# A fp32 decoder layer on one core: MLP operands two pairs to an instruction, norm scratch and load order changed

## The chip, the core and the metric

The kernel runs on one core of a Trainium2 chip. The core has five engines, each with its own instruction queue: TensorE (PE), VectorE (DVE), ScalarE (ACT), GpSimd (POOL) and SyncE (SP, which here issues most DMA transfers). The metric is device time in microseconds for one launch, the median of the runs. All times in the text are microseconds unless marked ns.

## The reference, cut to what matters

One decoder layer, 2048 tokens of 1024 features, all in fp32. A token mixer comes first; it is not touched by the change. The rest is:

```python
x = x + merged @ w_o                                   # mixer: merged is its output
h = rmsnorm(x, g_mlp)
x = x + jnp.square(jax.nn.relu(h @ w_ff1)) @ w_ff2     # 1024 -> 4096 -> 1024
h = rmsnorm(x, g_ple)
x = x + jax.nn.sigmoid(h @ w_ple_gate) * (p @ w_ple_proj)
return rmsnorm(x, g_final)
```

## The kernel before

**Splitting.** Every fp32 operand of a product is split into a rounded part and a remainder (`split`, L1101 to L1103): ACT casts (L1102), then DVE or POOL subtracts the cast from the source (L1103). `mm3` (L133) makes a product from three matmuls: high by high, high by low, low by high. So each 128x512 operand costs one ACT instruction and one DVE or POOL instruction, which stand in the profile as `op<-hr`, `op<-w` and so on under L1102 and L1103.

**Seven products.** Both MLP products are done by a scheme with seven instead of eight half-size products, P1 to P7, on sums and differences of the blocks. The tokens are two blocks (`blk`) of 1024. The combinations of the activations are called A11, A12, S1, S2, S3, A22 and S4, those of the weights are formed by a subtraction in place, and the order is P1, P2, P5, P6, P7, P4, P3.

**First product (about 1660 to 2390).** For each block 16 pairs of column tiles; a pair (`pair`) has 84 matmuls, 12 to each of the seven products. The activations stand split in SBUF (`home`: hA, hS, yx, big), the weight operands come from `combine`. The additions and the squared ReLU after it (L1276, L1282) run on DVE and POOL on tiles of the ring `t2` (7 buffers), and the results go to DRAM (`rD`, L1288). While block 0's pairs run, `heads1` prepares block 1: it loads x (`hr`, a ring of two buffers, L1108), normalizes it (`norm_tile`: a Square on ACT with its sum, L160, the result going to an unused tile `junk` that is taken from the t2 ring; a chain of small DVE instructions for the reciprocal root, L165 and L149 to L155; a DVE product, L173), transposes it on PE (L137), and puts the combinations into DRAM (`hD`). At the last pair of block 0 `fill_home` loads these into `hr` and splits them into the home tiles, as soon as the last matmul on each is done: half on DVE, half on POOL, 128x1024 each.

**Second product (about 2390 to 3041).** For each block four chunks of the 4096 hidden columns, in each chunk seven products: 56 steps of 48 matmuls. For the step after the present one, `operands` loads the activations (`hr`, 1 MB, L1367), splits them on ACT and POOL, forms the weight combination from `w` tiles (L1375 for P5, L1377 for P6, L1379 for P7, L1381 for P4, all on POOL) and splits it on ACT and DVE; four pairs (activations, weights) to a step, each pair one tile of the ring `op`, of 6 + 10 tiles, that is, two steps. The weights come as 64 loads of 512 KB (`load_w2`, L1354). Each product is added to its accumulators `accP` (L1440 on ACT for first chunks, else L1442 on DVE); in the last chunk of a block the accumulators are combined (L1448) and put to DRAM (`x2D`, L1451), for block 1 from ACT's queue. The accumulators of P2, P4 and P3 start from the residual (`accP<-x1D`, L1420), loaded at the first P1 of a block. PSUM: a step uses four `d` banks or two `rp` and two `rc`, by turns.

**Gate stage (3041 to the end).** Gate weights are loaded (L1488) and split to `wg`, the input is normalized (`norm_in`, L1395, L160, L173) and turned (`turn_in`), then gate, embedding and the last norm.

**What sets the order.** PE's order is the order in which the code is written. That of DVE, ACT, POOL and SP is set by a scheduler when the kernel is built, which may hoist an instruction: the first two `norm_in` of the gate stage, written near the end of the second product, stand on DVE at the switch from block 0 to block 1. Each engine works through its own row in order; an instruction that waits holds all that stand behind it.

Of the kernel before, what the change touches and what calls it, by code (L numbers as in the profile page):

```python
# [98 lines left out]
def hybrid_kernel(ctx, tc, consts, x, p, g_mix, w_in, mu_shift, w0, w_decay_up, a0, w_aaa_up,  # L99
# [101 lines left out]
    with ExitStack() as c1:  # L201
# [886 lines left out]
        ring = dict(n=0, a=6, b=6)  # L1088

        def optile():  # L1090

            n = ring["n"] % (ring["a"] + ring["b"])
            ring["n"] += 1
            if n < ring["a"]:
                return hx.tile([P, 2, 512], FR, name="op", tag="op", bufs=ring["a"])
            return ring["pool"].tile([P, 2, 512], FR, name="op", tag="op", bufs=ring["b"])
# [66 lines left out]
        def combine(pool, pr, wrb, tmp):  # L1163
# [10 lines left out]
            def op(nm, src, eng):  # L1174
                t = optile().rearrange("p s (k n) -> p s k n", n=P)
                split((t[:, 0], t[:, 1]), src, eng)
                ops[nm] = t
# [88 lines left out]
    def prod(ops, nm, last):  # L1266
        ps = pps()
        h = home[FIRST[nm]]
        for k in range(4):
            mm3(ps, (ops[nm][:, 0, k, :], ops[nm][:, 1, k, :]), (h[:, 0, k, :], h[:, 1, k, :]), k == 0, k == 3)  # L1270
        if last:
            fill_home(FIRST[nm])
        return ps
# [71 lines left out]
    ring.update(pool=f3, b=10, n=0)  # L1345
    w2v = w_ff2[0].rearrange("(k p) c -> p k c", p=P)
    lo, hi = slice(0, 512), slice(512, D)

    def load_w2(c):
        w = {}  # L1350
        for e in range(2):
            for p_ in range(KC):
                w[p_, e] = g3.tile([P, D], F32, name="w2", tag="w2", bufs=12)
                SP.dma_start(out=w[p_, e], in_=w2v[:, 2 * (c * KC + p_) + e, :])  # L1354
        return w
# [9 lines left out]
    def operands(blk, c, nm, w):  # L1365
# [3 lines left out]
        for p_ in range(KC):  # L1369
            a = optile()  # L1370
            split((a[:, 0, :], a[:, 1, :]), raw[:, p_, :], POOL)
            e, o = w[p_, 0], w[p_, 1]
            b11, b12, b21, b22 = e[:, lo], e[:, hi], o[:, lo], o[:, hi]
            if nm == "P5":
                POOL.tensor_tensor(b11, b12, b11, ALU.subtract)  # L1375
            elif nm == "P6":
                POOL.tensor_tensor(b11, b22, b11, ALU.subtract)  # L1377
            elif nm == "P7":
                POOL.tensor_tensor(b12, b22, b12, ALU.subtract)  # L1379
            elif nm == "P4":  # L1380
                POOL.tensor_tensor(b21, b21, b11, ALU.subtract)  # L1381
# [8 lines left out]
    hts, xts = {}, {}  # L1390
# [21 lines left out]
    for n, (blk, c, nm) in enumerate(seq):  # L1412
        cur = nxt
        g = blk * NCH + c
        if nm == "P1":
            if c == 0:

                for a, e, ns in (("P2", 0, lo), ("P4", 1, lo), ("P3", 0, hi)):
                    for j in range(4):
                        SP.dma_start(out=accs[a][j], in_=x1D[rows_of(blk, e, j), ns])  # L1420
# [3 lines left out]
        if n + 1 < len(seq):  # L1424
# [4 lines left out]
            nxt = operands(b_, c_, nm_, w2[b_ * NCH + c_])  # L1429
        pss = [dps() for _ in range(4)] if n % 2 == 0 else [rps(), rps(), cps(), cps()]  # L1430
# [6 lines left out]
        for j in range(4):  # L1437
# [12 lines left out]
            def put(k, e, ns):  # L1450
                (ACT if blk + 1 == NBLK else SP).dma_start(out=x2D[rows_of(blk, e, j), ns], in_=s[k])  # L1451
# [28 lines left out]
    wgv = w_ple_gate[0].rearrange("(k p) c -> p k c", p=P)  # L1480
    wpv = w_ple_proj[0].rearrange("(k p) c -> p k c", p=P)
# [3 lines left out]
    def weights(view, res, pool, n, ks, nm):  # L1485

        raw = hr()
        SP.dma_start(out=raw[:, 0:len(ks), :], in_=view[:, ks[0]:ks[-1] + 1, (lo, hi)[n]])  # L1488
# [118 lines left out]
```

## Time and profile before

| | us |
|---|---|
| runs | 3300.75, 3304.99, 3310.25; median 3304.99 |
| profiled execution | 3303.2 |
| its span | 3301.4 |
| PE busy in the span | 3054.8 (93%) |
| DVE, POOL, ACT busy | 2455.9 (74%), 1653.8 (50%), 1336.2 (40%) |

The profile is of one execution. A row of the order of time reads: start, length, engine, line, operation, output <- inputs, shapes, count of merged instructions, and in brackets how long the engine had been idle and what released it. A row of the list of waits reads: who waited, for which engine's which tile and line, total, times, longest. L numbers are lines of the kernel before; the helpers `split` and `mm3` appear under their own lines.

### The profile page before, as it was taken

Reading aid. Unit: us, or ns where it says so; the run is one execution under the profiler, and the core shown is the slowest. Engines: PE = TensorE matmul, PEld = TensorE weight load, DVE = VectorE, ACT = ScalarE, POOL = GpSimd, SP = SyncE. Lnnn points to the kernel's source line nnn. Section 1 sums busy time; section 2 is a strip of 40 time slices with the busy share of each in tenths; the row PEclk is TensorE's granted clock in tenths of the full one; section 3 lists DMA queues with packets and bytes.
Section 4 is the critical chain, followed back from the end, with each engine's and each line's share of the span. In section 5 each row is a group of like instructions: output and inputs, shape, how many; then the busy total and the mean of one; then the engine's idle time right before and its main releaser. Section 6 shows DMA issues by size and latency. Waiting matters only on the chain. (4 is left out here: it accounts for less than half of the span.)

```text
span 3301.4 us, 44294 instructions
## 1 busy us (share of the span) xinstructions
PE 3054.8 (93%) x14409; PEld 2492.0 (75%) x14409; DVE 2455.9 (74%) x5424; ACT 1336.2 (40%) x2774; POOL 1653.8 (50%) x1657
## 2 busy tenths in 40 slices
PE   7999989999999998788989889899989998999998
PEld 6777777777878786677777667688878886887787
DVE  4479888788888878875477777776657697668665
ACT  4445655455455444432233223222244434443332
POOL 4545444444334434531245456655589887885000
PEclk9999999999999999899999999899999999999999
DMA  7876767765666567767755455544464464335331
GB/s 246 241 225 196 244 202 233 237 216 192 216 211 218 188 205 238 246 213 264 273 193 177 148 177 190 181 153 147 169 227 153 142 217 177 141 128 177 127 115 67
DMA packets 423219, 636.41 MB, mean 193 GB/s; under 512 B 174222, under 2 KB 286412, under 8 KB 391756
## 3 DMA queue, kind: packets, MB, share of 16 engines
q1 hardware_dynamic: 420684, 629.39, 57.7%
q10 hardware_dynamic: 2304, 4.20, 0.3%
q8 instruction: 114, 1.87, 0.2%
q14 instruction: 117, 0.96, 0.1%
HBM read 439.49 MB, written 193.99 MB: 192 GB/s over the span
## 5 line engine op out<-in xcount | busy, mean ns | idle before, releaser
L133 PE MATMUL d<-big,wf 128*128 128x512 f32 (+1 forms) x3288 | 849.7, 406 | 19.1 <-DVE wf L244 8.9
L133 PEld LDWEIGHTS d<-big,wf 128*128 128x128 f32 x3288 | 609.5, 192 | 157.7 <-DVE wf L244 11.4
L1103 DVE TENSOR_TENSOR op<-w,op 128x512 fp32r<-128x512 f32 x224 | 287.4, 1295 | 139.2 <-ACT op L1102 137.8
L1103 POOL TENSOR_TENSOR op<-hr,op 128x512 fp32r<-128x512 f32 x224 | 331.2, 1494 | 95.5 <-ACT op L1102 95.5
L133 PE MATMUL d<-op 128*128 128x512 f32 x1344 | 314.6, 393 | 12.6 <-POOL op L1103 8.9
L133 PEld LDWEIGHTS d<-op 128*128 128x128 f32 x1344 | 253.4, 189 | 69.2 <-POOL op L1103 9.3
L1102 ACT CAST op<-hr 128x512 fp32r<-128x512 f32 x224 | 139.3, 622 | 323.2 <-PE rc L133 109.8
L872 DVE TENSOR_TENSOR Xtmp<-Xt,At 128x16 f32<-128x16 f32 (+15 forms) x512 | 242.8, 474 | 9.3
L1103 POOL TENSOR_TENSOR op<-wr,op 128x512 fp32r<-128x512 f32 x96 | 141.5, 1483 | 206.3 <-ACT op L1102 206.3
L133 PE MATMUL d<-yx,wf 128*128 128x512 f32 x768 | 206.9, 416 | 22.7 <-ACT yx L390 15.7
L133 PE MATMUL d<-wf,big 128*128 128x512 f32 x768 | 200.8, 415 | 26.1 <-DVE t2k L611 13.8
L133 PE MATMUL d<-wg,op 128*128 128x512 f32 x768 | 187.0, 399 | 11.3 <-ACT wg L1102 11.0
L133 PEld LDWEIGHTS d<-wf,big 128*128 128x128 f32 x768 | 146.6, 196 | 64.1 <-DVE t2k L611 17.4
L1276 POOL TENSOR_TENSOR t<-t,t 128x512 f32<-128x512 f32 x128 | 189.4, 1490 | 9.8 <-issue 5.6
L133 PEld LDWEIGHTS d<-yx,wf 128*128 128x128 f32 x768 | 147.3, 198 | 59.8 <-ACT yx L390 17.4
L133 PE MATMUL rp<-op 128*128 128x512 f32 x672 | 173.5, 393 | 13.9 <-DVE accP L1442 12.3
L133 PEld LDWEIGHTS d<-wg,op 128*128 128x128 f32 x768 | 147.1, 192 | 46.4 <-ACT wg L1102 11.6
L1102 ACT CAST op<-wr 128x512 fp32r<-128x512 f32 x192 | 110.0, 618 | 166.9 <-DMA wr<-in_w_ff_dram 113.1
L133 PE MATMUL rc<-op 128*128 128x512 f32 x672 | 171.7, 391 | 0.0
L244 POOL TENSOR_TENSOR wf<-wr,wf 128x640 fp32r<-128x640 f32 (+2 forms) x69 | 120.5, 1747 | 78.5 <-ACT wf L241 74.3
L133 PEld LDWEIGHTS rp<-op 128*128 128x128 f32 x672 | 126.9, 190 | 42.0 <-issue 12.7
L875 DVE TENSOR_REDUCE Xt<-Xtmp 128x8 f32<-128x16 f32 (+15 forms) x512 | 147.3, 288 | 9.2
(319 smaller groups left out, 6396.4 us busy)
## 6 DMA issues: line engine op xcount, KB each, us to landing
wf<-wc SPq DMA_DIRECT2D x131, 1024.0 KB, 5.4
wc<-wf SPq DMA_DIRECT2D x50, 1024.0 KB, 6.3
wr<-in_w_ff_dram SPq DMA_DIRECT2D x64, 512.0 KB, 4.4
w<-in_w_ff_dram SPq DMA_DIRECT2D x64, 512.0 KB, 4.2
wr<-in_w_in_dram SPq DMA_DIRECT2D x51, 512.0 KB, 4.3
zD<-t2k SPq DMA_DIRECT2D x96, 256.0 KB, 3.9
zs<-zD SPq DMA_DIRECT2D x32, 640.0 KB, 6.4
At<-aD SPq DMA_DIRECT2D x32, 512.0 KB, 5.1
```

What stands on the lines that cost most here:

```text
L133: PE.matmul(out_, lhsT, rhs, start=start, stop=stop, **kw)
L244: eng.tensor_tensor(wf[:, 1, c], raw[:, c], hi.bitcast(F32)[:, c], ALU.subtract)
L872: DVE.tensor_tensor(tmp[:, :, :, 0:n], Xt[:, :, 0:n].unsqueeze(2).broadcast_to([P, MCOL, FS, n]), At[:, 0:n, r:n].rearrange("p s r -> p r ...
L875: DVE.tensor_reduce(Xt[:, :, r:n].unsqueeze(3), tmp[:, :, :, 0:n], AX.X, ALU.add)
L1102: ACT.copy(out=dst[0], in_=src)
L1103: eng.tensor_tensor(dst[1], src, dst[0].bitcast(F32), ALU.subtract)
L1276: eng.tensor_tensor(out_, a, b, op)
```

## The change

1. The ring `op` has tiles of twice the size and half their number (3 + 3 in the first product, 3 + 5 in the second). In the first product two operands share a tile (`ophalf`). In the second, `operands` treats two pairs at once: casts, subtractions and weight combinations are 128x1024 instead of 128x512, half as many. The weight loads are 32 of 1 MB.
2. The weight combinations of P5 and P6 move from POOL to DVE; those of P7 and P4 stay on POOL.
3. `fill_home` runs at high priority, and gives DVE 128x1024 and 128x512, POOL 128x512.
4. The norm of `heads1` squares in two halves into a scratch tile of its own (`jk`), with one more DVE addition of the two sums (L1125), and no longer takes a tile of the t2 ring. Its product is now L1126.
5. The residual loads of P4 and P3 move from the first P1 to the first P6 of a block.
6. Block 1's stores to `x2D` are issued by SP instead of ACT.
7. The first raw gate weights are loaded in the last but one step (`graws`); `turn_in` uses one double tile.

```diff
-        ring = dict(n=0, a=6, b=6)
+        ring = dict(n=0, a=3, b=3)
...
-                norm_tile(pool, x_, gb, x_, junk)
+                if junk:
+                    norm_tile(pool, x_, gb, x_, junk)
+                    continue
+                ss = pool.tile([P, 2], F32, name="nss2", bufs=2)
+                for n in range(2):
+                    jk = pool.tile([P, 512], BF16, name="jk", bufs=1)
+                    ACT.activation(out=jk, in_=x_[:, n * 512:(n + 1) * 512], func=AF.Square, accum_out=ss[:, n:n + 1])
+                DVE.tensor_tensor(ss[:, 0:1], ss[:, 0:1], ss[:, 1:2], ALU.add)
+                DVE.scalar_tensor_tensor(x_, x_, rstd(pool, ss[:, 0:1], 1, "n"), gb, op0=ALU.mult, op1=ALU.mult)
...
-        for k, eng in ((slice(0, 2), DVE), (slice(2, 4), POOL)):
-            split((home[nm][:, 0, k, :], home[nm][:, 1, k, :]), raw[:, k, :], eng)
+        with tc.high_priority():
+            for k, eng in ((slice(0, 2), DVE), (slice(2, 3), DVE), (slice(3, 4), POOL)):
+                split((home[nm][:, 0, k, :], home[nm][:, 1, k, :]), raw[:, k, :], eng)
...
-            xt = normed(1, j, f2, [t[:, 0, :], t[:, 1, :]], dict(tag="t2", bufs=NT2))
+            xt = normed(1, j, f2, [t[:, 0, :], t[:, 1, :]], None)
...
-        for p_ in range(KC):
+        for q in range(KC // 2):
             a = optile()
-            split((a[:, 0, :], a[:, 1, :]), raw[:, p_, :], POOL)
+            split((a[:, 0], a[:, 1]), raw[:, 2 * q:2 * q + 2, :], POOL)
...
             if nm == "P5":
-                POOL.tensor_tensor(b11, b12, b11, ALU.subtract)
+                DVE.tensor_tensor(b11, b12, b11, ALU.subtract)
             elif nm == "P6":
-                POOL.tensor_tensor(b11, b22, b11, ALU.subtract)
+                DVE.tensor_tensor(b11, b22, b11, ALU.subtract)
...
-        if nm == "P1":
-            if c == 0:
-                for a, e, ns in (("P2", 0, lo), ("P4", 1, lo), ("P3", 0, hi)):
+        if c == 0:
+            for a, e, ns in dict(P1=[("P2", 0, lo)], P6=[("P4", 1, lo), ("P3", 0, hi)]).get(nm, ()):
...
+        if n + 2 == len(seq):
+            graws += [raw_weights(wgv, 0, ks) for ks in (range(4), range(4, 8))]
...
-                (ACT if blk + 1 == NBLK else SP).dma_start(out=x2D[rows_of(blk, e, j), ns], in_=s[k])
+                SP.dma_start(out=x2D[rows_of(blk, e, j), ns], in_=s[k])
```

How the rows of the engines move, at three places. First DVE in block 0's pairs, at the norm for the second head of block 1. Before, the small instructions of the norm (nmsn, rs_...) stand behind the last additions and ReLUs of a pair (t tiles):

```order
L1282 SCALAR_TENSOR_TENSOR t_18031<-t_18031 128x512
L1276 TENSOR_TENSOR t_17973<-t_17973,d 128x512
L1282 SCALAR_TENSOR_TENSOR t_17973<-t_17973 128x512
L1276 TENSOR_TENSOR t_17942<-t_17942,d 128x512
L1103 TENSOR_TENSOR op<-wr,op 128x512
L1282 SCALAR_TENSOR_TENSOR t_17942<-t_17942 128x512
L165 TENSOR_SCALAR nmsn<-nss 128x1
L149 TENSOR_SCALAR rs_yn<-nmsn 128x1
L151 TENSOR_SCALAR rs_hn<-nmsn 128x1
L150 TENSOR_SCALAR rs_yn<-rs_yn 128x1
L153 TENSOR_TENSOR rs_qn<-rs_yn 128x1
L154 TENSOR_TENSOR rs_qn<-rs_qn,rs_hn 128x1
```

After, the same norm begins one pair earlier, behind the last ReLUs of the pair before, among the additions of the previous head (L1168, L1172; L1151 and L1155 of before, where they stand 21 rows ahead of the norm):

```order
L1292 TENSOR_TENSOR t_17755<-t_17755,d 128x512
L1298 SCALAR_TENSOR_TENSOR t_17755<-t_17755 128x512
L1125 TENSOR_TENSOR nss_18065<-nss_18065 128x1
L165 TENSOR_SCALAR nmsn<-nss_18065 128x1
L149 TENSOR_SCALAR rs_yn<-nmsn 128x1
L151 TENSOR_SCALAR rs_hn<-nmsn 128x1
L150 TENSOR_SCALAR rs_yn<-rs_yn 128x1
L153 TENSOR_TENSOR rs_qn<-rs_yn 128x1
L154 TENSOR_TENSOR rs_qn<-rs_qn,rs_hn 128x1
L1168 TENSOR_TENSOR t_17906<-t_17889,hr 128x512
L155 SCALAR_TENSOR_TENSOR rs_yn<-rs_qn,rs_yn 128x1
L1172 TENSOR_TENSOR t_17911<-t_17906,hr 128x512
```

So the norm has moved ahead by about the rows of one pair on DVE, and the casts of the next pair's weights stand behind its Square on ACT.

Second, POOL at the entry to the second product: `op<-hr` are P1's and P2's activation operands, `t` the last additions of the first product, and `w` weight combinations. Before:

```order
L1375 TENSOR_TENSOR w_22428<-w_22428 128x512
L1276 TENSOR_TENSOR t_22392<-t_22344,t_22372 128x512
L1103 TENSOR_TENSOR op<-hr,op 128x512
L1375 TENSOR_TENSOR w_22430<-w_22430 128x512
L1375 TENSOR_TENSOR w_22432<-w_22432 128x512
L1276 TENSOR_TENSOR t_22344<-t_22311,t_22344 128x512
L1276 TENSOR_TENSOR t_22397<-t_22392,t_22311 128x512
L1379 TENSOR_TENSOR w_22428<-w_22436,w_22428 128x512
L1379 TENSOR_TENSOR w_22430<-w_22438,w_22430 128x512
L1379 TENSOR_TENSOR w_22432<-w_22440,w_22432 128x512
L1276 TENSOR_TENSOR t_22416<-t_22313,t_22397 128x512
L1103 TENSOR_TENSOR op<-hr,op 128x512 x2
```

After:

```order
L1112 TENSOR_TENSOR op<-hr,op 128x1024
L1292 TENSOR_TENSOR t_22318<-t_22270,t_22298 128x512
L1292 TENSOR_TENSOR t_22270<-t_22237,t_22270 128x512
L1292 TENSOR_TENSOR t_22323<-t_22318,t_22237 128x512
L1112 TENSOR_TENSOR op<-hr,op 128x1024
L1292 TENSOR_TENSOR t_22342<-t_22239,t_22323 128x512
L1396 TENSOR_TENSOR w_22354<-w_22358,w_22354 128x2x512
L1112 TENSOR_TENSOR op<-hr,op 128x1024 x3
L1396 TENSOR_TENSOR w_22356<-w_22360,w_22356 128x2x512
L1398 TENSOR_TENSOR w_22358<-w_22358,w_22354 128x2x512
```

P5's combinations (L1375) are gone from POOL, and P7's (L1379, now L1396) have moved behind the second and last operand of P1; an `op<-hr` row is now two pairs.

Third, DVE at the switch from block 0 to block 1: the norms of the gate stage (rs_..., xt), and the additions of P2's product to its accumulators. Before:

```order
L153 TENSOR_TENSOR rs_qn<-rs_yn 128x1
L154 TENSOR_TENSOR rs_qn<-rs_qn,rs_hn 128x1
L1103 TENSOR_TENSOR op<-w_24506,op 128x512
L155 SCALAR_TENSOR_TENSOR rs_yn<-rs_qn,rs_yn 128x1
L153 TENSOR_TENSOR rs_qn<-rs_yn 128x1
L154 TENSOR_TENSOR rs_qn<-rs_qn,rs_hn 128x1
L155 SCALAR_TENSOR_TENSOR rs_yn<-rs_qn,rs_yn 128x1
L173 SCALAR_TENSOR_TENSOR xt<-xt,rs_yn,gb 128x1024
L1442 TENSOR_TENSOR accP_22448<-accP_22448,rp 128x512
L1103 TENSOR_TENSOR op<-w_24508,op 128x512
L1442 TENSOR_TENSOR accP_22449<-accP_22449,rp 128x512
```

After:

```order
L154 TENSOR_TENSOR rs_qn<-rs_qn,rs_hn 128x1
L153 TENSOR_TENSOR rs_qn<-rs_yn 128x1
L1112 TENSOR_TENSOR op<-w_24084,op 128x1024
L155 SCALAR_TENSOR_TENSOR rs_yn<-rs_qn,rs_yn 128x1
L154 TENSOR_TENSOR rs_qn<-rs_qn,rs_hn 128x1
L1467 TENSOR_TENSOR accP_22366<-accP_22366,rp 128x512
L173 SCALAR_TENSOR_TENSOR xt<-xt,rs_yn,gb 128x1024
L155 SCALAR_TENSOR_TENSOR rs_yn<-rs_qn,rs_yn 128x1
L1467 TENSOR_TENSOR accP_22367<-accP_22367,rp 128x512
L1467 TENSOR_TENSOR accP_22368<-accP_22368,rc 128x512
L1467 TENSOR_TENSOR accP_22369<-accP_22369,rc 128x512
L173 SCALAR_TENSOR_TENSOR xt<-xt,rs_yn,gb 128x1024
```

In both the chains of the two norms stand ahead of the first addition of P2's product (accP<-accP,rp). After, the two chains are interleaved, and the two products with g (L173) stand behind the first and behind the fourth addition, where both stood ahead of all four.

More of the change, by code (lines that the diff above doesn't have):

```diff
@@ L1094, in optile, with ophalf @@
             if n < ring["a"]:
-                return hx.tile([P, 2, 512], FR, name="op", tag="op", bufs=ring["a"])
-            return ring["pool"].tile([P, 2, 512], FR, name="op", tag="op", bufs=ring["b"])
+                return hx.tile([P, 2, 2, 512], FR, name="op", tag="op", bufs=ring["a"])
+            return ring["pool"].tile([P, 2, 2, 512], FR, name="op", tag="op", bufs=ring["b"])
+        half = []
+        def ophalf():
+            if not half:
+                t = optile().rearrange("p s x (k n) -> p s x k n", n=P)
+                half.extend((t[:, 0, x], t[:, 1, x]) for x in range(2))
+            return half.pop(0)
         def hr(shape=(P, 4, 512)):
@@ L1174, in op @@
             def op(nm, src, eng):
-                t = optile().rearrange("p s (k n) -> p s k n", n=P)
-                split((t[:, 0], t[:, 1]), src, eng)
-                ops[nm] = t
+                ops[nm] = ophalf()
+                split(ops[nm], src, eng)
             op("P1", b11, DVE)
@@ L1237, in hybrid_kernel @@
     SP.dma_start(out=raw, in_=w1v[:, 4:8, P:2 * P])
-    t = optile().rearrange("p s (k n) -> p s k n", n=P)
-    split((t[:, 0], t[:, 1]), raw, POOL)
-    ops_next["P3"] = t
+    ops_next["P3"] = ophalf()
+    split(ops_next["P3"], raw, POOL)
     USE = ("A11", "S2", "A12", "S3", "S1", "A22", "S4")
@@ L1269, in prod @@
         for k in range(4):
-            mm3(ps, (ops[nm][:, 0, k, :], ops[nm][:, 1, k, :]), (h[:, 0, k, :], h[:, 1, k, :]), k == 0, k == 3)
+            mm3(ps, (ops[nm][0][:, k, :], ops[nm][1][:, k, :]), (h[:, 0, k, :], h[:, 1, k, :]), k == 0, k == 3)
         if last:
@@ L1344, in hybrid_kernel @@
     f3 = c3.enter_context(tc.tile_pool(name="f3", bufs=1, side="left", reuse_waits="tile"))
-    ring.update(pool=f3, b=10, n=0)
-    w2v = w_ff2[0].rearrange("(k p) c -> p k c", p=P)
+    ring.update(pool=f3, b=5, n=0)
+    w2v = w_ff2[0].rearrange("(q x e p) c -> p q e x c", x=2, e=2, p=P)
     lo, hi = slice(0, 512), slice(512, D)
@@ L1351, in load_w2 @@
         for e in range(2):
-            for p_ in range(KC):
-                w[p_, e] = g3.tile([P, D], F32, name="w2", tag="w2", bufs=12)
-                SP.dma_start(out=w[p_, e], in_=w2v[:, 2 * (c * KC + p_) + e, :])
+            for q in range(KC // 2):
+                w[q, e] = g3.tile([P, 2, D], F32, name="w2", tag="w2", bufs=6)
+                SP.dma_start(out=w[q, e], in_=w2v[:, c * KC // 2 + q, e])
         return w
@@ L1368, in operands @@
         res = []
-        for p_ in range(KC):
+        for q in range(KC // 2):
             a = optile()
-            split((a[:, 0, :], a[:, 1, :]), raw[:, p_, :], POOL)
-            e, o = w[p_, 0], w[p_, 1]
-            b11, b12, b21, b22 = e[:, lo], e[:, hi], o[:, lo], o[:, hi]
+            split((a[:, 0], a[:, 1]), raw[:, 2 * q:2 * q + 2, :], POOL)
+            e, o = w[q, 0], w[q, 1]
+            b11, b12, b21, b22 = e[:, :, lo], e[:, :, hi], o[:, :, lo], o[:, :, hi]
             if nm == "P5":
-                POOL.tensor_tensor(b11, b12, b11, ALU.subtract)
+                DVE.tensor_tensor(b11, b12, b11, ALU.subtract)
             elif nm == "P6":
-                POOL.tensor_tensor(b11, b22, b11, ALU.subtract)
+                DVE.tensor_tensor(b11, b22, b11, ALU.subtract)
             elif nm == "P7":
@@ L1382, in operands @@
             b = optile()
-            split((b[:, 0, :], b[:, 1, :]), dict(P1=b11, P2=b21, P5=b11, P6=b11, P7=b12, P4=b21, P3=b22)[nm], DVE)
-            res.append((a, b))
+            split((b[:, 0], b[:, 1]), dict(P1=b11, P2=b21, P5=b11, P6=b11, P7=b12, P4=b21, P3=b22)[nm], DVE)
+            res += [(a[:, :, x], b[:, :, x]) for x in range(2)]
         return res
@@ L1388, in rows_of, with raw_weights @@
         return slice(blk * TC + e * 512 + j * P, blk * TC + e * 512 + (j + 1) * P)
-    hts, xts = {}, {}
+    wgv = w_ple_gate[0].rearrange("(k p) c -> p k c", p=P)
+    wpv = w_ple_proj[0].rearrange("(k p) c -> p k c", p=P)
+    hts, xts, graws = {}, {}, []
+    def raw_weights(view, n, ks):
+        raw = hr()
+        SP.dma_start(out=raw[:, 0:len(ks), :], in_=view[:, ks[0]:ks[-1] + 1, (lo, hi)[n]])
+        return raw
     def norm_in(j, pool, bufs):
@@ L1400, in turn_in @@
         xt = xts.pop(j)
-        hts[j] = ht = [hx.tile([P, 2, 512], FR, name="op", tag="op", bufs=ring["a"]).rearrange(
-            "p s (k t) -> p (s k) t", t=P) for _ in range(2)]
+        ht = hx.tile([P, 2, 2, 512], FR, name="op", tag="op", bufs=ring["a"])
+        hts[j] = ht = [ht[:, s_].rearrange("p x (k t) -> p (x k) t", t=P) for s_ in range(2)]
         for h in range(2):
@@ L1414, in hybrid_kernel @@
         g = blk * NCH + c
-        if nm == "P1":
-            if c == 0:
-                for a, e, ns in (("P2", 0, lo), ("P4", 1, lo), ("P3", 0, hi)):
-                    for j in range(4):
-                        SP.dma_start(out=accs[a][j], in_=x1D[rows_of(blk, e, j), ns])
+        if c == 0:
+            for a, e, ns in dict(P1=[("P2", 0, lo)], P6=[("P4", 1, lo), ("P3", 0, hi)]).get(nm, ()):
+                for j in range(4):
+                    SP.dma_start(out=accs[a][j], in_=x1D[rows_of(blk, e, j), ns])
         if nm == "P5" and g + 1 < NBLK * NCH:
@@ L1479, in hybrid_kernel @@
     f4 = ctx.enter_context(tc.tile_pool(name="f4", bufs=1, side="left", reuse_waits="tile"))
-    wgv = w_ple_gate[0].rearrange("(k p) c -> p k c", p=P)
-    wpv = w_ple_proj[0].rearrange("(k p) c -> p k c", p=P)
     wgs, wps, pts, xs, fss = {}, {}, {}, {}, {}
@@ L1485, in weights @@
     def weights(view, res, pool, n, ks, nm):
-        raw = hr()
-        SP.dma_start(out=raw[:, 0:len(ks), :], in_=view[:, ks[0]:ks[-1] + 1, (lo, hi)[n]])
+        raw = graws.pop(0) if graws else raw_weights(view, n, ks)
         for i, k in enumerate(ks):
```

## The prediction

> **What bounds the kernel now.** I read the page first, then busy time by stage, then the list of what TensorE (PE) waited for, and only then the order of time around the longest waits. The page gives the span of the profiled execution.
>
> ```profile
> span 3301.4 us, 44294 instructions
> ```
>
> That execution took 3303.2 us in all, so 1.8 us lie outside the span; the median of the three runs shown is 3304.99, another 1.8 above it. Next, busy time by stretch: start and end, length, then for PE, PEld, DVE, ACT and POOL busy time and instruction count, PE's granted clock (1.00 is full), DMA share and GB/s.
>
> ```profile
> 1700.00:2380.00 680.00, 633.94 (x2712) 511.37 (x2711) 494.06 (x695) 174.34 (x298) 394.48 (x261) 0.96 0.50 165
> 2450.00:2730.00 280.00, 280.00 (x1232) 230.80 (x1231) 216.83 (x226) 118.63 (x212) 242.59 (x160) 1.00 0.50 177
> 1820.00:1840.00 20.00, 7.84 (x30) 6.00 (x29) 15.22 (x22) 3.29 (x6) 10.92 (x7) 0.66 0.44 145
> 2050.00:2100.00 50.00, 33.16 (x108) 23.98 (x107) 45.70 (x38) 18.14 (x25) 40.70 (x22) 0.80 0.74 253
> 2388.00:2408.00 20.00, 11.10 (x48) 8.79 (x48) 14.51 (x11) 5.30 (x10) 19.53 (x13) 0.86 0.87 336
> 2730.00:2762.00 32.00, 16.03 (x63) 12.24 (x62) 29.98 (x39) 16.74 (x32) 24.89 (x19) 0.82 0.42 156
> 3036.00:3070.00 34.00, 21.76 (x70) 14.81 (x69) 29.39 (x64) 17.41 (x33) 14.87 (x10) 0.75 0.68 248
> ```
>
> The second row is the steady part of the second product: PE is busy for 280.00 of 280 us at clock 1.00, 1232 matmuls, 0.227 us each. There nothing can be gained, whatever becomes cheaper on DVE or POOL. All there is to gain lies in the last five rows, five places where PE stops. Which wait ends last there, over 1700 to 3301 (total, times, longest):
>
> ```profile
> PE d L137 <- DVE hr L173: 28.8, 6, 10.2
> PE rp L133 <- DVE accP L1442: 12.3, 1, 12.3
> PE d L133 <- ACT wg L1102: 11.0, 2, 6.3
> PE d L133 <- POOL op L1103: 8.9, 1, 8.9
> PE rc L133 <- DVE big L1103: 5.4, 1, 5.4
> PE d L133 <- DVE yx L1103: 2.7, 1, 2.7
> PE rp L133 <- DVE hS L1103: 2.7, 1, 2.7
> PE rc L133 <- ACT big L1102: 2.4, 1, 2.4
> ```
>
> In this order: the norms of block 1's heads (row 1), the switch from block 0 to block 1 in the second product (2), the entry to the gate stage (3), the entry to the second product (4), and the refill of the home tiles at the start of block 1's pairs (5 to 8). The stages ahead of 1660 are not touched, and stay.
>
> **(a) Norms of the heads.** Around the second of them, on ACT, on DVE and on PE:
>
> ```profile
> 1812.73 1.06 ACT L160 ACTIVATE junk<-hr 128x1024 bf16<-128x1024 f32 x1 [1.99 <-POOL t L1276]
> ```
> ```profile
> 1833.01 2.25 DVE L173 SCALAR_TENSOR_TENSOR hr<-hr,rs_yn,gb 128x1024 f32<-128x1024 f32 x1
> ```
> ```profile
> 1835.41 1.09 PE L137 MATMUL d<-ident,hr 128*128 128x128 f32 x4 [10.19 <-DVE hr L173]
> 1836.14 4.50 PE L133 MATMUL d<-hA,op 128*128 128x512 f32 x12
> 1840.48 2.96 PE L133 MATMUL d<-hS,op 128*128 128x512 f32 x12
> ```
>
> The Square on ACT writes its unused result into a tile of the t2 ring, and is released by POOL's last use of that tile, not by its own data. From it a chain of small DVE instructions runs to L173 at 1835.3, and PE stands for 10.19 us. The change gives the Square a scratch tile of its own, so it waits for the load alone, and in the new order of DVE the norm stands about one pair (84 matmuls, 19 us at 0.227) earlier. The longest of the six waits is 10.2, so all six should go: 28.8 us. Behind each of the two long ones PE also ran slowly: 12 matmuls took 4.50 where the next 12 took 2.96, 1.5 us each time. Added: two half Squares for one, and one 1-column add, on ACT (3.29 of 20 us busy here) and on DVE, some 0.3 us hidden by those 19 us. If only the two long waits shrink to the size of the short ones (about 2 us), 16 us go. I take **-29**, between -16 and -33 (28.8 + 2 x 1.5, and some of the slow start behind the short ones).
>
> **(b) Refill of the home tiles.** The fourth of the seven refills on DVE and on POOL, and PE at the last:
>
> ```profile
> 2066.04 1.21 DVE L1103 TENSOR_TENSOR yx<-hr,yx 128x1024 fp32r<-128x1024 f32 x1
> ```
> ```profile
> 2062.89 2.68 POOL L1103 TENSOR_TENSOR yx<-hr,yx 128x1024 fp32r<-128x1024 f32 x1 [2.44 <-ACT yx L1102]
> ```
> ```profile
> 2087.38 0.51 PE L133 MATMUL rc<-big,op 128*128 128x512 f32 x1 [2.44 <-ACT big L1102]
> 2093.28 5.06 PE L133 MATMUL rc<-big,op 128*128 128x512 f32 x11 [5.40 <-DVE big L1103]
> ```
>
> By count, 50 us should hold 220 matmuls and hold 108: 25 us are lost, at clock 0.80. POOL starts its half of yx at 2062.89, so ACT's cast is there by then, and DVE comes 3.1 us later, because pair work stands ahead of it. In the new order each refill is one 128x1024 and one 128x512 on DVE, standing together, and POOL has only 128x512, half of 2.68. The last refill moves ahead of some eight pair operations: ACT's cast is there at 2087.38, DVE's half, 1.21 us of work, at 2093.28, so 4.7 us of it are queue. That 4.7, 2.7 for yx and some 1 us each for the three others that wait make 10. Against it: half as much again on DVE per refill, 0.6 us, on an engine busy for 45.70 of 50 us, and two hr buffers still feed seven loads. I take **-10**, between -2 and -18 (the loads keep at least a quarter of the 25).
>
> **(c) Entry to the second product.** POOL while PE waits 8.9 us for an operand that POOL begins in the last row:
>
> ```profile
> 2393.53 3.44 POOL L1375 TENSOR_TENSOR w<-w 128x512 f32<-128x512 f32 x2
> 2396.92 3.40 POOL L1276 TENSOR_TENSOR t<-t,t 128x512 f32<-128x512 f32 x2
> 2400.29 4.60 POOL L1379 TENSOR_TENSOR w<-w,w 128x512 f32<-128x512 f32 x3
> 2404.85 1.26 POOL L1276 TENSOR_TENSOR t<-t,t 128x512 f32<-128x512 f32 x1
> 2406.06 2.50 POOL L1103 TENSOR_TENSOR op<-hr,op 128x512 fp32r<-128x512 f32 x2
> ```
>
> Subtractions for P5 (L1375) and P7 (L1379), needed much later, stand ahead of P1's operand: 8.04 us. In the new order P5's are on DVE and P7's come behind P1's operand; three t additions stay ahead of it. P5's activations no longer queue on SP behind eight residual loads. 8.04 would take nearly the whole wait, but one instruction of 128x1024 now makes two operands, so the first comes later than it could; and the next wait, DVE's split of the weights, isn't seen. I take **-7**, from 0 to -12 (20 us less 48 x 0.227 is 9.1 lost, and 3 us more at the bank changes after it).
>
> **(d) Block switch.** P6 of the first chunk waits 12.3 us for DVE's P2 additions, which stand behind two norms that the scheduler put there for the gate stage. DVE and POOL grouped, 2730 to 2760, and in the last fence the same small operation between 3047 and 3058 (busy us, mean ns, idle before):
>
> ```profile
> L155 DVE SCALAR_TENSOR_TENSOR rs_yn<-rs_qn,rs_yn 128x1 f32<-128x1 f32 x6 | 7.3, 1218 | 0.2
> L154 DVE TENSOR_TENSOR rs_qn<-rs_qn,rs_hn 128x1 f32<-128x1 f32 x6 | 6.2, 1026 | 0.2
> L153 DVE TENSOR_TENSOR rs_qn<-rs_yn 128x1 f32<-128x1 f32 x6 | 6.0, 1001 | 0.2
> ```
> ```profile
> L1103 POOL TENSOR_TENSOR op<-hr,op 128x512 fp32r<-128x512 f32 x11 | 14.3, 1318 | 0.0
> L1377 POOL TENSOR_TENSOR w<-w,w 128x512 f32<-128x512 f32 x4 | 5.9, 1482 | 3.3 <-DVE op L1103 2.6 <-DVE rs_qn L154 0.7
> L1381 POOL TENSOR_TENSOR w<-w,w 128x512 f32<-128x512 f32 x4 | 5.1, 1278 | 0.0
> ```
> ```profile
> L155 DVE SCALAR_TENSOR_TENSOR rs_yn<-rs_qn,rs_yn 128x1 f32<-128x1 f32 x6 | 1.0, 159 | 0.2
> ```
>
> One column takes 1218 ns beside POOL, about the length of one POOL instruction, and 159 ns without it: 19.5 us for 18 operations that need 2.9. The new order keeps both norms ahead of the P2 additions, interleaved, with 17 of the 18 small operations, two subtractions for P6 (L1394, two SBUF inputs) and a split ahead of the first addition; one of the two L173 goes behind all four. What POOL has to do in this stretch is what it can make DVE wait: 25.3 us before, 5.9 less without P6's subtractions, and 2 x 1.21 or more goes to DVE. 5.9 + 2.25 for that L173, less about 2 x 2.3 for the subtractions, is 3.6. I take **-4**. If POOL has done its work before the norms start, the whole 12.3 and the slow clock go (-14); if all 17 meet a POOL instruction of twice the length, they take 17 x (2.56 - 1.08) = 25 more (twice 1278 ns, against 19.5 / 18), less 5.9 and 2.25: +17.
>
> The Trainium skill, "SBUF — State Buffer", section "Who interferes with whom", says that a DVE instruction with two SBUF inputs and a GpSimd instruction that reads SBUF take the shared port for a whole instruction, the later one standing still. That speaks against doubling POOL's instructions: the term would be +17. The rows agree on the lock (1218 beside 159), but bound it by POOL's work.
>
> **(e) Gate entry.** ACT's first gate casts, the load of the second gate weights on SP, and the PE wait on it:
>
> ```profile
> 3041.02 4.26 ACT L1102 CAST wg<-hr 128x512 fp32r<-128x512 f32 x8 [6.03 <-DVE accP L1448]
> ```
> ```profile
> 3048.62 0.38 SPq L1488 DMA_DIRECT2D hr<-in_w_ple_gate_dram  x1
> ```
> ```profile
> 3058.95 7.28 PE L133 MATMUL d<-wg,op 128*128 128x512 f32 x16 [6.33 <-ACT wg L1102]
> ```
>
> ACT stood behind its own stores, which wait for DVE's last additions; these go to SP, and the casts can start about 4 us earlier. DVE's half of the splits still follows the additions, and POOL runs beside it, so PE gains 1 to 3. On SP the 12 stores now stand ahead of loads issued before 3041, so the 3048.62 load can slip by as much. I take **-2**, between -8 and +4.
>
> **The rest** I cost at nothing: 1 MB weight loads for two of 512 KB (the same bytes, in a stretch with DMA share 0.50), half as many ACT, DVE and POOL instructions for the operands, the residual loads of P4 and P3 moved to P6 (needed at P4's additions, over two steps later). Their cover is the 280.00 of 280: it holds as long as DVE (216.83, plus the 29 subtractions of this stretch that move, 18 to 35 us as 128x1024) and POOL (242.59, less 29 x 1.48 = 43) stay below 280.
>
> **Sum:** 29 + 10 + 7 + 4 + 2 = 52. 3303.2 - 52 = 3251; put on the median, 1.8 more: **3253 us**.
>
> **Rivals.** 1. *Only the norms gain.* The new heads' norm frees PE, but refill and entries are bound by loads (DMA share 0.74 to 0.87 there) and keep their waits, and the switch loses a little: -29 - 2 + 6 = -25, 3280. For it: two hr buffers as before; against it: POOL began yx 3.1 us before DVE. 2. *The norm's wait is replaced.* The new Square is free early, but the chain behind it still meets POOL on every small operation (1.2 us instead of 0.16) and is late again; POOL is busy for 394.48 of 680 us. Then (a) is -5, the rest -5: 3295. Against it: 19 us of lead. 3. *Slower: DVE becomes the bound of the second product.* For P5 and P6 in a row, DVE now has 4 subtractions and 4 splits of 1.21; if each first waits for a POOL instruction of 2.56, that is 8 x 3.77 = 30 in two steps of 48 x 0.227 = 10.9, 21.8 together: 8.4 short per chunk, 67 over 8 chunks, 3320. It decides once 7.8 us per chunk are not made good, since 8 x 7.8 = 62 outweighs the 52 by 10. Against it: DVE has 63 of 280 us idle, five of seven products bring it no subtraction, and operands are made one product ahead.
>
> **How the numbers follow.** Forecast 0.60 (3226 to 3270), rival 1 0.24 (3270 to 3290), rival 2 0.10 (3288 to 3305), rival 3 0.06. The terms' bounds don't all fall one way; 3226 is the forecast with (a), (b) and (c) near their far ends and (d) half way. From 3226 to 3288 lie the forecast and nearly all of rival 1. A measurement tells about 0.3% (10 us) from no change, so faster means below 3295: forecast, rival 1 and a third of rival 2, 0.87; same 0.07; slower 0.06.
>
> **What would show it.** Right: no wait of PE on the heads' norm left over 3 us between 1700 and 2000; the list of waits shorter by the five long ones; PE still 280 of 280 within the second product. Wrong in (a): the wait there again, with the Square early and L173 late. Wrong in (d): the wait on the P2 additions as long or longer, with small DVE operations of about 2.4 us. Rival 3: PE waiting for a DVE split or subtraction in P5 or P6 of every chunk.

## The result, and the profile after

The change takes 3283.33 us (median of 5 runs, 3278.03 to 3291.36), the kernel before 3309.76 (5 runs); the ratio of the means is 0.9931, 95% interval 0.9909 to 0.9953. That is faster, by 23 us (16 to 30; the medians lie 26 apart), where 52 were forecast. A further set of runs of the same kernel gave 0.9919 (0.9901 to 0.9936). First the head of the page after:

```profile
span 3289.5 us, 43492 instructions
```

The profiled execution (3291.36) is the slowest of its five, so I don't compare spans but stages, cut where PE starts on something that both kernels have: block 0's first matmul of the first product (`d<-hA`), the first of the second product (`d<-op`), P2's first (`rp<-op`), and the end.

| stage | before | after | difference | forecast |
|---|---|---|---|---|
| up to block 0's first matmul (not touched) | 1700.1 | 1710.6 | +10.5 | 0 |
| first product, terms (a) and (b) | 689.6 | 651.9 | -37.7 | -39 |
| entry to the second product, (c) | 22.2 | 33.7 | +11.5 | -7 |
| from P2's first matmul to the end, (d) and (e) | 889.6 | 893.4 | +3.8 | -6 |

The first line is chance: in the second profiled execution of the changed kernel that stage ended at 1704.5, and in the experiments between 1700.2 and 1707.6. The other three lines came out there as 651.3, 33.3 and 893.0. Together they make -22.4, which is what the means show. So (a) and (b) were met in sum, and 28 of the missing 30 us were lost in (c) and behind it.

The stretches of after that answer to those shown of before (same columns): the refill, the entry, steady second product, block switch, steady again, gate entry.

```profile
2040.00:2100.00 60.00, 53.91 (x221) 42.06 (x220) 52.68 (x58) 20.45 (x34) 40.21 (x26) 0.97 0.66 225
2362.00:2397.00 35.00, 15.55 (x55) 11.87 (x54) 18.81 (x10) 9.15 (x12) 23.99 (x11) 0.71 0.81 311
2450.00:2695.00 245.00, 245.00 (x1071) 200.69 (x1069) 193.74 (x168) 89.56 (x90) 150.62 (x56) 1.00 0.48 162
2695.00:2745.00 50.00, 38.89 (x151) 29.62 (x150) 45.12 (x57) 18.47 (x25) 30.36 (x12) 0.90 0.56 192
2770.00:3000.00 230.00, 230.00 (x1006) 188.51 (x1005) 176.76 (x147) 83.65 (x84) 146.88 (x54) 1.00 0.40 135
3018.00:3058.00 40.00, 21.74 (x70) 16.07 (x69) 30.87 (x64) 16.14 (x31) 15.53 (x10) 0.70 0.64 233
```

The refill now runs at clock 0.97 where it had 0.80 (over 60 us instead of 50; over the 40 us from 2035 it is 0.96), and in the steady stretches PE is full as before, so nothing was lost there. The entry is the worst place now: 55 matmuls in 35 us, clock 0.71. The list of what PE waited for, 1700 to 3300, in the changed kernel:

```profile
PE d L133 <- ACT op L1111: 15.3, 1, 15.3
PE d L133 <- DVE wg L1112: 11.1, 3, 6.5
PE rp L133 <- DVE accP L1467: 7.6, 2, 7.5
PE d L133 <- DVE op L1112: 5.1, 2, 4.1
PE d L133 <- ACT wg L1111: 4.7, 1, 4.7
PE d L133 <- DVE t L1292: 4.7, 1, 4.7
PE rp L133 <- DVE big L1112: 3.9, 1, 3.9
PE rc L137 <- DVE xt L173: 2.4, 1, 2.4
PE d L133 <- ACT hr L1163: 2.1, 2, 1.9
PE d L133 <- DVE accP L1467: 2.0, 1, 2.0
PE d L137 <- DVE t L1292: 1.6, 1, 1.6
PE rc L133 <- DVE accP L1467: 1.4, 1, 1.4
```

The heads' norm (28.8) is gone, the four long waits of the refill are down to 3.9 and what is under 1, and the switch from 12.3 to 7.5. But other waits are new: 15.3 and 4.1 (the first and the fourth row) at the entry, and 11.1 on DVE's gate weights beside 4.7 on ACT's, where the kernel before waited 11.0 on ACT's.

**The entry, read from the trace.** PE, ACT and SP of the changed kernel, where the second product begins:

```profile
2362.47 5.62 PE L133 MATMUL d<-op 128*128 128x512 f32 x24
2383.41 0.80 PE L133 MATMUL d<-op 128*128 128x512 f32 x1 [15.33 <-ACT op L1111]
2388.32 7.98 PE L133 MATMUL d<-op 128*128 128x512 f32 x23 [4.11 <-DVE op L1112]
```
```profile
2358.83 1.05 ACT L1111 CAST op<-w 128x1024 fp32r<-128x1024 f32 x1 [11.04 <-DMA w<-in_w_ff_dram]
2359.78 1.04 ACT L1111 CAST op<-hr 128x1024 fp32r<-128x1024 f32 x1
2380.42 1.04 ACT L1111 CAST op<-hr 128x1024 fp32r<-128x1024 f32 x1 [19.59 <-DMA hr<-rD0S]
2381.37 1.99 ACT L1111 CAST op<-w 128x1024 fp32r<-128x1024 f32 x2
```
```profile
2369.91 0.32 SPq L1384 DMA_DIRECT2D hr<-rD0S  x1
```

PE does the first half of P1 (24 matmuls) and stands. What it needs is the cast of P1's second weights, the second of the two at 2381.37. In ACT's row stand ahead of it the casts of P5's first activations and weights, and the former waits 19.6 us for a load that SP issues at 2369.91. ACT is idle all that time. Half of the wait passes before the load is issued, the other 10.5 us while it is under way; in those the DMA engines move 411 GB/s. ACT's row in the changed program, with the buffer numbers of `w` (22354 and 22356 are the first and second tile of the half that P1 uses):

```
L1111 CAST op<-w_22354 128x1024
L1111 CAST op<-hr 128x1024 x2
L1111 CAST op<-w_22354 128x1024
L1111 CAST op<-w_22356 128x1024
```

The second `op<-hr` and the second `op<-w_22354` are P5's, `op<-w_22356` is P1's. As I read the program, the cause lies in the tiles: of P1's four double tiles three are in the part of the ring that is there all the time, and the fourth, P1's second weights, is the first of the part that the scheduler gives out only once the first product's last results are on their way. P5's first tile is free as soon as P1's first half is done. With single tiles, six of eight were there all the time. The run with the tiles swapped, below, tests this.

**The gate entry.** SP, DVE and PE of the changed kernel:

```profile
3007.66 17.67 SPq L1476 DMA_DIRECT2D x2D<-accP  x12
...
3030.50 0.38 SPq L1413 DMA_DIRECT2D hr<-in_w_ple_gate_dram  x1
```
```profile
3020.93 4.05 DVE L1473 TENSOR_TENSOR accP<-accP,accP 128x512 f32<-128x512 f32 x3
3024.91 2.48 DVE L1112 TENSOR_TENSOR wg<-hr,wg 128x512 fp32r<-128x512 f32 x4
```
```profile
3025.64 8.41 PE L133 MATMUL d<-wg,op 128*128 128x512 f32 x23 [6.47 <-DVE wg L1112]
...
3042.50 0.80 PE L133 MATMUL d<-wg,op 128*128 128x512 f32 x1 [4.69 <-ACT wg L1111]
```

The twelve stores hold SP for 17.7 us, and the load of the second gate weights is issued 11.7 us after PE's first matmul of the gate stage (3018.78), where it was 6.9 before (3048.62 and 3041.69). ACT is free early, as forecast, and POOL begins its gate splits at 3017.96; but then DVE's last three additions, beside these splits, take 4.05, and the 6.47 of wait ends with DVE. In the kernel before, POOL was idle at that time, and the three took 1.89:

```profile
3038.73 1.89 DVE L1448 TENSOR_TENSOR accP<-accP,accP 128x512 f32<-128x512 f32 x3
```

### The profile page after: what moved, and what is told of

It is laid out like the page before. It is cut to its first block, busy times and chain, and to the rows that moved or that the text cites. A ratio compares the mean times of both kernels' runs of the same rounds, so it can differ in the third digit from the quotient of the medians.

```text
span 3289.5 us, 43492 instructions
## 1 busy us (share of the span) xinstructions
PE 3056.5 (93%) x14409; PEld 2493.0 (76%) x14409; DVE 2496.4 (76%) x5359; ACT 1317.0 (40%) x2573; POOL 1522.9 (46%) x1449
## 5 line engine op out<-in xcount | busy, mean ns | idle before, releaser
L133 PE MATMUL d<-big,wf 128*128 128x512 f32 (+1 forms) x3288 | 851.5, 407 | 17.2 <-DVE wf L244 9.7
L1112 POOL TENSOR_TENSOR op<-hr,op 128x1024 fp32r<-128x1024 f32 x112 | 297.5, 2664 | 173.4 <-ACT op L1111 173.4
L1112 DVE TENSOR_TENSOR op<-w,op 128x1024 fp32r<-128x1024 f32 x112 | 228.8, 2047 | 158.2 <-ACT op L1111 158.2
L133 PE MATMUL d<-op 128*128 128x512 f32 x1344 | 319.1, 396 | 21.5 <-ACT op L1111 15.3
L1111 ACT CAST op<-hr 128x1024 fp32r<-128x1024 f32 x112 | 117.6, 1050 | 376.3 <-PE rc L133 120.6
L133 PE MATMUL d<-wg,op 128*128 128x512 f32 x768 | 187.4, 400 | 15.8 <-DVE wg L1112 11.1
```

Of the source, the lines that this page charges most:

```text
L133: PE.matmul(out_, lhsT, rhs, start=start, stop=stop, **kw)
L1111: ACT.copy(out=dst[0], in_=src)
L1112: eng.tensor_tensor(dst[1], src, dst[0].bitcast(F32), ALU.subtract)
```

## The experiments

Each was timed against the kernel before in the same set of runs, in which its median lay between 3306.42 and 3309.76; the ratios, of the means, are what can be compared between rows. The stages of their profiled executions, cut as above:

| kernel | first product | entry | from P2 to the end | median | ratio (95% interval) |
|---|---|---|---|---|---|
| before | 689.6 | 22.2 | 889.6 | 3309.76 | 1 |
| after | 651.9 | 33.7 | 893.4 | 3283.33 | 0.9931 (0.9909 to 0.9953) |
| norm alone | 666.1 | 22.1 | 889.1 | 3284.04 | 0.9931 (0.9918 to 0.9945) |
| refill alone | 682.6 | 22.2 | 890.2 | 3298.38 | 0.9972 (0.9961 to 0.9983) |
| norm and refill | 658.8 | 22.2 | 891.9 | 3277.85 | 0.9914 (0.9899 to 0.9928) |
| double tiles, P5 and P6 on DVE | 682.6 | 33.8 | 888.3 | 3307.77 | 1.0003 (0.9992 to 1.0014) |
| after, tiles swapped | 650.8 | 24.2 | 891.8 | 3275.98 | 0.9906 (0.9891 to 0.9922) |
| after, stores on ACT | 652.4 | 32.8 | 889.0 | 3275.26 | 0.9907 (0.9893 to 0.9921) |
| after, P5 and P6 on POOL | 651.5 | 30.8 | 885.1 | 3275.45 | 0.9906 (0.9890 to 0.9922) |
| both repairs, first P7 on DVE | 649.5 | 17.5 | 889.8 | 3267.06 | 0.9881 (0.9865 to 0.9897) |
| the same, P5 and P6 on POOL | 651.6 | 17.2 | 885.0 | 3259.17 | 0.9853 (0.9836 to 0.9869) |

**The norm alone.** The kernel before with this:

```diff
-            xt = normed(1, j, f2, [t[:, 0, :], t[:, 1, :]], dict(tag="t2", bufs=NT2))
+            xt = normed(1, j, f2, [t[:, 0, :], t[:, 1, :]], None)
```

and the branch of `normed` for it.

> The kernel before with part 4 of the change alone: the heads' norm squares into a scratch tile of its own. Theory: the six waits of PE on the heads' norm (28.8 us) go, and little else moves; the first product, from block 0's first matmul to the second product's first (689.6 in the kernel before, 651.9 after the whole change), takes 658 to 664, and the time falls by 26 to 32 us, ratio about 0.991. Rival: the 37.7 of that stage come mostly from the refill of the home tiles; then this stage takes 675 or more and the ratio is above 0.996.

The stage fell by 23.5, to 666.1, just outside the range: the theory holds, its size was 5 too large. The ratio is that of the whole change. The waits on the norm are all gone, and some others have come. In the changed kernel, DVE and PE at the second head:

```profile
1822.79 1.22 DVE L155 SCALAR_TENSOR_TENSOR rs_yn<-rs_qn,rs_yn 128x1 f32<-128x1 f32 x1
1824.04 2.28 DVE L1126 SCALAR_TENSOR_TENSOR hr<-hr,rs_yn,gb 128x1024 f32<-128x1024 f32 x1
...
1834.96 0.68 DVE L1292 TENSOR_TENSOR t<-t,d 128x512 f32<-128x512 f32 x1
```
```profile
1829.98 1.03 PE L137 MATMUL d<-ident,hr 128*128 128x128 f32 x8
1835.69 5.26 PE L133 MATMUL d<-hA,op 128*128 128x512 f32 x12 [4.68 <-DVE t L1292]
```

The norm is ready at 1826.3, 3.7 us before PE starts on the head; I had counted on 19. Before that DVE did its chain (the last three small operations still 1.2 us each beside POOL) ahead of the pair's additions, so these come late, a `d` bank isn't free, and PE waits 4.7 for the addition at 1834.96 and starts slowly again: 12 matmuls in 5.26. In the kernel with the norm alone the same wait is 4.65, and PE waits 8.0 us in all for such additions in block 0's pairs.

**The refill alone.** The kernel before with the three splits at high priority (three quarters on DVE).

> The kernel before with part 3 alone: the refill of the home tiles at high priority, three quarters on DVE. Theory: 8 to 12 us of the 25 lost there come back; the first product takes 678 to 682 of 689.6, ratio about 0.997. Rival (the refill is bound by its loads): 687 or more, ratio 0.999 to 1.001.

The stage fell by 7.0 us, to 682.6, just outside the theory's range and far from the rival's; the ratio is 0.9972. The refill isn't bound by its loads alone; my 10 was 3 too many.

**Norm and refill together.** Both edits in the kernel before.

> The kernel before with parts 3 and 4 alone, norm and refill. Apart they took 23.5 and 7.0 off the first product, the whole change 37.7. Theory: the two help one another (the refill begins with less behind it on DVE), so that the first product takes 650 to 655 and, with entry, second product and gate stage as before (22, 630, 260), the ratio is 0.987 to 0.990: under that of the whole change. Rival: the other 7 come from the double tiles; then the first product takes 657 to 661 and the ratio is 0.990 to 0.992.

30.8, the sum of 23.5 and 7.0: my theory that the two help one another fell, and the rival holds. The other 7 of the first product's 37.7 come with the double tiles, and at the refill: PE waits 2.6, 2.8 and 6.2 us there in this kernel, and 0.6, 3.9, 0.6 and 1.0 in the whole change. The ratio, 0.9914, is that of the whole change within the intervals: all that the rest of the change did was undone by what it cost.

**Double tiles alone.** Parts 1, 2 and 7 of the change; norm, refill, residual loads and stores as in the kernel before.

> Parts 1, 2 and 7 of the change alone (operands two pairs to an instruction, P5's and P6's combinations on DVE, gate weights); norm, refill, residual loads and stores as before. Theory: these bring the loss at the entry and little else: first product 683 to 690, entry 31 to 35, second product 622 to 629, gate stage 258 to 262; the time is within 6 us of the kernel before, ratio 0.998 to 1.002. Rival: the moved residual loads make the loss at the entry, not the double tiles; then the entry is 18 to 25 and the ratio 0.996 or less.

As expected at the entry: 33.8. So the loss there comes with the double tiles (about 3 of it with part 2, as the run with P5 and P6 on POOL shows below), and not with part 5, which this kernel doesn't have. The order of the loads on SP is not excluded by this run: the scheduler puts eight residual loads behind P5's load here too (from 2399.19, the load at 2396.52), where in the kernel before they stand ahead of it. The first product, 682.6, came out just below the expected range, 7.0 shorter than before, though its pairs' operands have the same size. The gain lies at the refill, where PE waits 8.3 us in all (the longest 5.2) and waited 16.8 before. What in the order makes that I haven't found. The time is that of the kernel before, 1.0003: -7 and +11.6 and a little.

**The tiles swapped.** The whole change with:

```diff
+        tiles = [optile() for _ in range(4)]
         for q in range(KC // 2):
-            a = optile()
+            a, b = (tiles[0], tiles[1]) if q == 0 else (tiles[3], tiles[2])
...
-            b = optile()
```

P1's second weights now lie in the third tile, and its second activations in the fourth. P5's activations are loaded into the buffer of `hr` from which P1's are read, so they can't come before P1's second activations are done.

> The whole change, but of a step's four operand tiles the third goes to the second weights and the fourth to the second activations. P1's second weights then lie in a tile that is free early, and P5's activations can't be loaded before P1's second activations are read. Theory: the entry to the second product lost 11.5 us because in ACT's row P1's second weight cast stands behind P5's first cast, which waits 19.6 us for its load; with it ahead, the stretch from P1's first to P2's first matmul (22.2 in the kernel before, 33.7 after) takes 16 to 24, and the time is 9 to 17 us under that of the whole change. Rival: the 1 MB weight loads come late at over 400 GB/s, whatever ACT's row; then the stretch stays above 30 and the time within 3 us of the whole change.

The entry fell from 33.7 to 24.2, just above the range; the median is 7 us under after, where 9 to 17 were expected, with intervals that overlap. The weight loads are as large as in the whole change, so the rival is out. What is left is the next wait in line, on POOL; POOL and PE of this kernel:

```profile
2360.19 6.59 POOL L1397 TENSOR_TENSOR w<-w,w 128x1024 f32<-128x1024 f32 x2
2366.75 7.99 POOL L1112 TENSOR_TENSOR op<-hr,op 128x1024 fp32r<-128x1024 f32 x3
```
```profile
2370.12 7.14 PE L133 MATMUL d<-op 128*128 128x512 f32 x22 [10.47 <-POOL op L1112]
```

Two weight combinations for P7, not needed for 40 us, stand ahead of P1's second activations.

**The stores on ACT again.** The whole change with part 6 undone (one line).

> The whole change, but block 1's stores to x2D are issued by ACT again, as before. Theory: the gate stage became 11 us longer (259.7 before, 270.7 after) because SP held the loads for it behind the twelve stores; with the stores on ACT it takes 258 to 263, and the time is 8 to 12 us under that of the whole change. Rival: ACT's earlier casts set POOL's splits against DVE's last additions, and that is the larger part of the loss, or the two cost the same on either queue: 268 or more, the time within 3 us of the whole change.

The gate stage is back at 260.9, as the theory said, but only 4.4 of that is gain: with ACT held, PE begins the stage later, and from P2 to the end it is 889.0 against 893.4. The median is 8 under after, with overlapping intervals. So the stores on SP cost 4 to 5 us. Whether that is the loads held on SP, as I had it, or ACT's early casts, which bring POOL's splits beside DVE's last additions, this run doesn't tell: with the stores on ACT both are gone. The rest of the loss at the gate entry isn't explained by the stores: here PE waits 5.40, 2.29, 5.25 and 2.93 there, 15.9 us, and 12.1 in the kernel before.

**P5's and P6's combinations on POOL.** The whole change with part 2 undone (DVE to POOL in two lines).

> The whole change, but P5's and P6's weight combinations on POOL, as before. Theory: at the switch POOL has 5.9 us more that DVE's small norm instructions can meet, and 1 instruction of twice the length more for each: the wait of P6 grows from 7.5 to 11 to 14, and the second product from 622.6 to 626 to 630; steady PE stays full. The time is 3 to 10 us over that of the whole change. Rival: the move does nothing, since POOL is idle for more than that: second product within 2 us, time within 3.

The opposite: from P2 to the end 885.1, 8.2 us less than after, and the entry 2.9 less. Theory and rival both fell. Switch and block end in the changed kernel, and then in this one (PE rows with a wait):

```profile
2697.43 9.58 PE L133 MATMUL d<-op 128*128 128x512 f32 x39 [2.05 <-DVE accP L1467]
...
2710.46 0.96 PE L133 MATMUL rc<-op 128*128 128x512 f32 x3 [1.41 <-DVE accP L1467]
...
2738.52 1.62 PE L133 MATMUL rp<-op 128*128 128x512 f32 x3 [7.50 <-DVE accP L1467]
```
```profile
2705.03 2.50 PE L133 MATMUL rp<-op 128*128 128x512 f32 x5 [3.94 <-DVE op L1112]
...
2725.51 1.62 PE L133 MATMUL rp<-op 128*128 128x512 f32 x6 [1.10 <-DVE accP L1467]
```

With the subtractions DVE is late at the end of the block, where it also combines the accumulators: 2.0 and 1.4 us on accP. Without them the norms' small operations mostly found POOL idle and took 0.15 us, and P6 waited 1.1 us instead of 7.5. Of the 8.2 us, 3.5 lie ahead of P6's first matmul and 4.7 behind it.

**Both repairs, and P7's combination.** Tiles swapped, stores on ACT, and in the first chunk `(POOL if blk or c else DVE).tensor_tensor(b12, b22, b12, ALU.subtract)`.

> The whole change with both repairs (third operand tile to the second weights; block 1's stores on ACT) and a third: in the first chunk P7's weight combination is on DVE, since with the first repair alone PE still waited 10.5 us for P1's second activations, which stood on POOL behind two of these of 3.3 us each. Theory (the two losses are separate, and add): entry 16 to 19 (24.2 with the first repair alone), gate stage 259 to 262, first and second product as after the change; the time is 20 to 27 us under that of the whole change, ratio to the kernel before 0.985 to 0.988. Rival: the repairs meet the same limit, and PE waits for the next engine in line; then the ratio stays at 0.989 or above.

0.9881: the medians are 16 us under the whole change, less than the 20 to 27 expected. The entry is 17.5, as expected, 4.7 under the kernel before: PE's wait on POOL there is 3.9. From P2 to the end it is 889.8, as with the stores on ACT alone.

**The same with P5's and P6's combinations on POOL,** except in the first chunk:

> The repaired kernel (third tile to the second weights, block 1's stores on ACT, first chunk's P7 combination on DVE), and P5's and P6's combinations back on POOL except in the first chunk. With them on POOL the whole change gained 8 us, against what was expected. Theory now: DVE and not POOL is late where a block ends; without the subtractions PE no longer waits for additions into accP there (2.0, 1.4 and 8.3 us in the runs with them on DVE), at the price of some 4 us for a split at the switch. From P2's first matmul to the end 881 to 885 (889.8 with them on DVE), entry 16 to 19, first product 649 to 652; ratio to the kernel before 0.984 to 0.987. Rival: the gain was made by the order in which the stores and loads on SP happened to stand in that one kernel; then 888 to 892, ratio 0.988.

885.0 from P2 to the end, at the upper end of the range, entry 17.2, first product 651.6, ratio 0.9853: the theory holds, and this is the fastest kernel of all (3257.22 to 3261.25; the one above it 3266.31 to 3267.94). Its list of waits at the switch has 3.9 on the split and 1.9 on accP. Here the move to POOL gains 4.8 us from P2 to the end, and not 8.2; and 885.0 is what P5 and P6 on POOL gave with the stores still on SP (885.1). So this gain and that of the stores on ACT don't add.

**The whole change once more.**

> The whole change once more, on the same chip, for its profile: the profiled execution of it was the slowest of its five, and its mixing stage, which the change does not touch, ended 10.6 us later than that of the kernel before (1710.6 for 1700.1). Both theories: stages as before, first product 651 to 653, entry 32 to 35, from P2's first matmul to the end 892 to 895. If the 10.6 is chance, the first product begins between 1700 and 1710; if the change makes it, at 1709 or later again.

It began the first product at 1704.5, and the stages came out as expected (651.3, 33.3, 893.0): the change doesn't make the 10.6.

## Why the prediction was wrong

**What bounds the kernel** was right: what changed lies in or next to the five places where PE stops, and the steady parts stayed full.

**(a)** Right mechanism, term too large: 23.5 for 29. The norm did come 19 us earlier: its end is 135.2 us behind block 0's first matmul before, and 115.7 after. The step that was off is the price, which I put at some 0.3 us hidden by those 19. Some 10 of the 19 made up the lateness, and some 5 went because PE, rid of its earlier waits, comes sooner, so that the norm is only about 4 us ahead of PE; and the pair's additions, which now stand behind it, are late: 8.0 us of new waits with the norm alone, 4.65 of them followed by a slow start.

**(b)** 7.0 for 10; the wait at the last refill did go. Seven more came in the first product with the double tiles, which I had at nothing. So the sum of the stage, -37.7 for -39, is right partly by luck.

**(c)** This step failed: -7 became +11.5. I read POOL's row at the entry, and it did what I said (P7's behind P1's operand). I didn't read ACT's, where P5's cast stands ahead of P1's. There P5's cast waits 19.6 us for its load, with P1's behind it. The order of a row is fixed when the kernel is built, so this could be read without a run. That "P5's activations no longer queue on SP behind eight residual loads" I put down as good; whether it helps P5's cast to come first, no run shows. With that order mended, and P7 out of the way, the term is -4.7 (22.2 to 17.5).

**(d)** As forecast in size, partly by luck: the wait on the P2 additions fell by 4.8. DVE and POOL of the changed kernel at the switch:

```profile
2726.56 2.33 DVE L154 TENSOR_TENSOR rs_qn<-rs_qn,rs_hn 128x1 f32<-128x1 f32 x1
2728.81 0.15 DVE L153 TENSOR_TENSOR rs_qn<-rs_yn 128x1 f32<-128x1 f32 x1
2728.92 2.32 DVE L155 SCALAR_TENSOR_TENSOR rs_yn<-rs_qn,rs_yn 128x1 f32<-128x1 f32 x1
...
2735.95 0.15 DVE L154 TENSOR_TENSOR rs_qn<-rs_qn,rs_hn 128x1 f32<-128x1 f32 x1
```
```profile
2726.46 9.36 POOL L1112 TENSOR_TENSOR op<-hr,op 128x1024 fp32r<-128x1024 f32 x4
```

A small operation that meets POOL takes 2.3 us where it took 1.2, and once POOL's four splits are done at 2735.8 the rest take 0.15: the cost is bounded by POOL's work, as I had it, and not 17 times the longer instruction. Of the 17 small operations ahead of the first addition five took 2.1 to 2.3 us, and the operation behind each of these, which by its place in the order is of the other chain, took 0.14 or 0.15. By the lock of the Trainium skill ("SBUF — State Buffer", "Who interferes with whom") each wait is one whole instruction, and these rows agree (2.3 us beside splits of 2.34). How many waits there are hangs, as I read it, on the order of the rows; no run changes that order alone. The step that failed here is the credit for the moved subtractions: I gave their move 5.9 us of freed POOL time, less 4.6 for DVE. The runs show a loss: with them on POOL the stretch from P2 to the end is 8.2 us shorter in the whole change, and 4.8 in the repaired kernel.

**(e)** This step failed too: -2 became a loss. From P6's first matmul at the switch to the end is 542.0 us before (2759.43 to 3301.4) and 551.0 after (2738.52 to 3289.5), +9.0. The stores on SP are 4.6 of it: with them on ACT it is 546.3 (2730.86 to 3277.2). I had the load's slip in the upper bound (+4), and not DVE's last additions, two SBUF inputs each, meeting POOL's early splits (4.05 us for three, 1.89 before). The shares overlap: with P5 and P6 on POOL and the stores on SP it is 546.3 too (2725.51 to 3271.8). The other 4 or so stand in the double-tile kernel as well, which has the stores on ACT: 545.7 (2765.49 to 3311.2). So they come with parts 1, 2 or 7; with which of them stays open.

**The rivals.** The time is near rival 1 ("only the norms gain", 3280), but for another reason: refill and first product gained, and entry and gate entry lost. Rival 3 holds at the end of the first block only: DVE is late there by 2.0 and 1.4 us, and at the switch, not in every chunk (230.00 of 230 busy between).

## What to carry to other kernels

When a ring's tiles become larger and fewer, look in the row of every engine that fills them for what now stands ahead of the first operand that PE needs, and what that waits for: an engine works in order, and one cast that waits for a load holds all behind it. A part that moves work from one engine to another is best timed by itself: here the move from POOL to DVE cost 8 us inside a change that gained 23, and 5 in the repaired kernel. Cut the profiled execution at places that both kernels share before comparing; a stage that wasn't touched moved by 10 us.

## What the runs showed of the hardware

A one-column DVE operation with two SBUF inputs took 0.15 us with POOL idle, 1.2 beside POOL instructions of 1.25 to 1.3, and 2.1 to 2.3 beside those of 2.4. After a wait of 4.7 us PE needed 5.26 us for 12 matmuls, and 2.96 for the next 12; over the 35 us of the entry, with 19.4 us of waits in them, the granted clock was 0.71 where it is 1.00 in the stretch behind it.
